# Neighbourhood attention: score products over 128 rows, value products from split operands, summed on the vector engines

## Chip, cores, metric

One core of a Trainium2 chip runs the whole program in one launch. The metric is the device time of one execution, in microseconds (us). Of several runs the median is taken. A profile is one execution recorded by the hardware profiler.

## What is computed

The program computes two layers of a transformer block over 512 image tokens (a grid of 8 rows by 64 columns) and 256 context tokens, with a width of 1024. Each layer has three branches (neighbourhood attention, a pooling mixer, latent attention), a gated merge and a gated feed-forward part. The change touches the neighbourhood branch, which has 8 heads of 64. Every query sees 16 columns of the grid and all 256 context tokens:

```python
s_win = einsum('bjqhd,bkjchd->bhjqkc', q_r, k_nb) * scale
s_win = where(in_win, s_win + bias, -inf)
s_ctx = einsum('bjqhd,bnhd->bhjqn', q_r, k_ctx) * scale
p = softmax(concatenate([s_win, s_ctx], -1))
out = einsum('bhjqkc,bkjchd->bjqhd', p_win, v_nb) + einsum('bhjqn,bnhd->bjqhd', p_ctx, v_ctx)
```

In the first layer the context tokens attend to themselves with the same projections (`dense_attn`). In the second layer their output isn't needed. All arithmetic is float32.

## The kernel before

**Split operands.** Most products run in the type fp32r, in which TensorE reads a float32 operand in reduced form. To keep the accuracy an operand is written as hi + lo: hi is the value rounded to fp32r (a copy on ScalarE, ACT in the profile), lo is the rest (a subtraction on VectorE, DVE, or on GpSimd, POOL). `evac` (line 386) does this for a result in PSUM. A dense product is then three products: hi·lo, hi·hi and lo·hi (`mm3`, line 375).

**The neighbourhood stage** of a layer (lines 936 to 985) works on four pairs of heads p. For each pair, `na_proj` projects queries, values and keys. Each pair has two heads e, on rows 64e to 64e+63 of the 128 partitions. For head e the tile `qz` holds the hi part of the queries on the head's own 64 rows and the lo part on the other 64; `kz` holds the hi part of the keys on both halves; `kl` holds the lo part of the keys of both heads, one head on each half. `na_vt` turns the values (10 blocks of 128 tokens) so that tokens lie on partitions.

**A unit** is one head and one block j of 128 queries (`na_unit`, line 793). Four matmuls make 128 x 512 scores `S`: for each half (window, context) one of `qz` by `kl` over the head's 64 rows alone and one of `qz` by `kz` over 128 rows, which gives hi·hi and lo·hi together. Softmax follows on DVE and ACT, four transposes on TensorE (`tps`), a copy to SBUF on ACT (`PT`), and four plain float32 matmuls of 64 weight columns by 128 moving columns into `ops`. TensorE runs each plain float32 matmul as two recorded passes. All 8 units of a pair write one PSUM tile `ops`, which stays taken until the pair is through; then one `evac` writes `nahi` and `nalo`. There are 32 units in each layer, and 8 units for the context (`na_ctx_unit`, `Sc`, `opc`) in the first.

**Order.** TensorE's order is written when the program is built: `Sched` (line 54) keeps a model of when each operand is ready and interleaves three streams of units (priority 0) with the dense tasks of `dense` (priority 1): the projections of all pairs, the gates and the first compressed projections of latent attention (`cps`). When a unit's next step is not ready by the model, dense matmuls are put in. In the first layer a background stream (`ada_back`, line 430, tile `adacc`) also works on DVE through the whole stage. The orders of the other engines are made by the framework's scheduler. Each engine runs its own order strictly, and waits at an instruction whose operands are missing. PSUM has four one-bank tiles for the units (`p1`) and two double ones for the dense tasks (`mm`). SBUF has `QB` = 12 tiles for queries, keys and values: two pairs of 6.

Of the kernel before, what the change touches and what calls it, by code (L numbers as in the profile page):

```python
# [28 lines left out]
KGAP = 800.0  # L29
QB = 12  # L30
DRATE = 360.0
# [15 lines left out]
class Need:  # L47
    """What a step waits for: tiles that it reads, pools and tags of tiles that it will take."""

# [4 lines left out]
class Sched:  # L54
    """Interleaves generators on the tensor engine by a model of when each step's operands are there."""

# [185 lines left out]
def body(tc, I, out):  # L242
# [247 lines left out]
    def first2(w0, w1, mov, T, dst):  # L490
        """Two weight tiles against the tokens in the order in which these come."""
        ws = (w0.prep(), w1.prep())
        for _ in ws:
            dst.append(pmm.tile([128, 1024], F32, tag="mm", name="f2ps"))
        bounds = [(a, a + 256) for a in range(0, T, 256)]
        n = [0, 0]
        for a, b in bounds:
            tts = range(a // 128, b // 128)
            yield lambda: all(t in tokens for t in tts)
            yield Need(at=max(tokens[t] for t in tts) + sch.HOP)  # L500
            for q in range(2):
# [143 lines left out]
    for l in range(NL):  # L645
# [101 lines left out]
        def na_proj(p, which):  # L747
            def run(w):
# [3 lines left out]
                if which != "v":  # L752
                    z = [na.tile([128, 768], F32R, tag="qkv", bufs=QB, name=which + "z") for _ in range(2)]
                    lo = na.tile([128, 768], F32R, tag="qkv", bufs=QB, name="kl") if which == "k" else None
                    for e in range(2):
                        a, o = slice(64 * e, 64 * e + 64), slice(64 - 64 * e, 128 - 64 * e)
                        for src, place in segs(ps, T):
                            hi = place(z[e])
                            nc.scalar.copy(out=hi[a], in_=src[a])
                            if which == "q":  # L760
                                nc.vector.tensor_sub(out=hi[o], in0=src[a], in1=hi[a].bitcast(F32))
                            else:
                                nc.vector.tensor_sub(out=place(lo)[a], in0=src[a], in1=hi[a].bitcast(F32))
                        if which == "k":
                            nc.scalar.copy(out=z[e][o, :T], in_=z[e][a, :T])
                    qkvt[p, which] = (*z, lo) if lo is not None else tuple(z)
                    return
# [6 lines left out]
        def na_vt(p):  # L774
            def run(_):
                v = qkvt[p, "v"]
                vt = na.tile([128, 10, 128], F32, tag="vt", bufs=2, name="vt")
                srcs = [v[:, 8 * BAND0[j] + 128 * hf:8 * BAND0[j] + 128 * hf + 128] for j in range(4) for hf in range(2)]
                srcs += [v[:, SX + i * 128:SX + (i + 1) * 128] for i in range(2)]
                for i0 in range(0, 10, 4):  # L780
                    tp = ps1.tile([128, 512], F32, tag="p1", name="vtps")
                    n = min(4, 10 - i0)
                    for i in range(n):
                        tr(tp[:, i * 128:(i + 1) * 128], srcs[i0 + i])
                    nc.scalar.copy(out=vt[:, i0:i0 + n, :], in_=tp[:, :n * 128].rearrange("p (k c) -> p k c", k=n))
                qkvt[p, "vt"] = vt
# [4 lines left out]
        biast = {}  # L791

        def na_unit(p, e, j):
            Q, (kk, kl) = qkvt[p, "q"][e], (qkvt[p, "k"][e], qkvt[p, "k"][2])
            vt = qkvt[p, "vt"]
            rows = slice(64 * e, 64 * e + 64)
            if (p, e) not in biast:
                biast[p, e] = na.tile([128, 3, 256], F32, tag="bias", bufs=2, name="bt")
                nc.sync.dma_start(out=biast[p, e], in_=I["rpbg"][l, 2 * p + e])
            if p not in opst:  # L800
                opst[p] = ps1.tile([128, 512], F32, tag="p1", name="ops")
                left[p] = 8
            bt, ops = biast[p, e], opst[p]
            S = ps1.tile([128, 512], F32, tag="p1", name="S")
            for c0 in (0, 256):
                k0 = 8 * BAND0[j] if c0 == 0 else SX
                q = slice(128 * j, 128 * j + 128)
                mm(out=S[:, c0:c0 + 256], lhsT=Q[rows, q], rhs=kl[rows, k0:k0 + 256], start=True, stop=False)
                mm(out=S[:, c0:c0 + 256], lhsT=Q[:, q], rhs=kk[:, k0:k0 + 256], start=False, stop=True)
# [13 lines left out]
            yield Need([P], [P1])  # L823
            tp = transpose_n(P, 4)
            PT = na.tile([128, 512], F32, tag="PT", bufs=3, name="PT")
            nc.scalar.copy(out=PT, in_=tp)
            yield Need([PT])
            for i in range(4):
                iv = 2 * j + i if i < 2 else 6 + i
                mm(out=ops[rows, j * 128:(j + 1) * 128], lhsT=vt[:, iv, rows], rhs=PT[:, i * 128:(i + 1) * 128],  # L830
                   start=i == 0, stop=i == 3)
            left[p] -= 1
            if left[p] == 0:
                evac(ops.rearrange("p (b r c) -> p b r c", b=8, r=8), rowm(nahi[:, p, :SX]), rowm(nalo[:, p, :SX]))
            yield 0

        def na_ctx_unit(p, e):
            Q, (kk, kl) = qkvt[p, "q"][e], (qkvt[p, "k"][e], qkvt[p, "k"][2])
            vt = qkvt[p, "vt"]
            rows = slice(64 * e, 64 * e + 64)  # L840
            S = ps1.tile([128, 512], F32, tag="p1", name="Sc")
            for qt in range(2):
                c, q = slice(qt * 256, (qt + 1) * 256), slice(SX + qt * 128, SX + (qt + 1) * 128)
                mm(out=S[:, c], lhsT=Q[rows, q], rhs=kl[rows, SX:768], start=True, stop=False)
                mm(out=S[:, c], lhsT=Q[:, q], rhs=kk[:, SX:768], start=False, stop=True)
# [11 lines left out]
            yield Need([P], [P1])  # L857
            tp = transpose_n(P, 4)
            PT = na.tile([128, 512], F32, tag="PT", bufs=3, name="PTc")
            nc.scalar.copy(out=PT, in_=tp)  # L860
            yield Need([PT], [P1])
            opc = ps1.tile([128, 512], F32, tag="p1", name="opc")
            for qt in range(2):
                for i in range(2):
                    mm(out=opc[rows, qt * 128:(qt + 1) * 128], lhsT=vt[:, 8 + i, rows],
                       rhs=PT[:, (2 * qt + i) * 128:(2 * qt + i + 1) * 128], start=i == 0, stop=i == 1)
            evac(opc[rows, 0:256], nahi[rows, p, SX:768], nalo[rows, p, SX:768])
            yield 0
# [117 lines left out]

        # latent attention: compressed streams, then the neighbourhood branch joins the sum
        mes = ExitStack()
# [380 lines left out]

        # gated feed-forward  # L1370
        h2 = (mhi, mlo)
# [268 lines left out]
```

## Time and profile before

| | us |
|---|---|
| median of 3 runs (lowest, highest) | 2567.89 (2561.16, 2567.93) |
| span of the profiled execution | 2567.5 |
| TensorE matmuls busy | 2481.2 (97%) |
| DVE busy | 1434.2 (56%) |
| ACT busy | 999.1 (39%) |
| POOL busy | 586.4 (23%) |
| neighbourhood stage, first layer | about 204 to 548 |
| neighbourhood stage, second layer | about 1626 to 1907 |

The busy time of TensorE is the time in which at least one matmul is recorded as running. Matmuls are pipelined, so a single one is listed longer than the step from its start to the start of the next. The cost of a matmul to a busy TensorE is this step, which the timeline shows.

### The profile page before, as it was taken

To read this page: it belongs to the slowest core of one execution; us is meant where nothing else is said; L and a number is where in the kernel's file an instruction comes from. 1 tells how busy PE (TensorE), PEld (TensorE's weight loads), DVE (VectorE), ACT (ScalarE), POOL (GpSimd) and SP (SyncE) were. 2 spreads that over 40 slices of the span, in tenths; PEclk is the share of its full clock that TensorE was granted. 3 is DMA by queue.
4 is the path that set the end of the run, shared out by engine and by line. 5 is a ranking of instruction groups with operands and counts; after the bars stand their busy time and mean duration, and the time that the engine had idled before them with its cause. 6 is when DMAs were issued, how large, how long until landed. Compare 5 with 4: busy or idle time off the path is not lost. (4 is left out here: it accounts for less than half of the span.)

```text
span 2567.5 us, 33598 instructions
## 1 busy us (share of the span) xinstructions
PE 2481.2 (97%) x13060; PEld 2056.5 (80%) x13060; DVE 1434.2 (56%) x2299; ACT 999.1 (39%) x1756; POOL 586.4 (23%) x413
## 2 busy tenths in 40 slices
PE   8899999999999999999999989999999998999998
PEld 6788788788887788888888867877787887888886
DVE  7645544554478668666673475333344785544444
ACT  5213443422467334322222333344423773433332
POOL 4301011142212224222221142101132122222212
PEclk9899999999999999999999999999999999999999
DMA  6343233223333544444431144212124335332322
GB/s 237 103 137 113 77 100 98 97 87 119 110 77 101 193 141 132 134 138 129 135 105 60 51 143 135 98 61 80 62 89 138 100 113 175 125 104 94 99 82 82
DMA packets 98598, 285.91 MB, mean 111 GB/s; under 512 B 12324, under 2 KB 13732, under 8 KB 98440
## 3 DMA queue, kind: packets, MB, share of 16 engines
q1 hardware_dynamic: 98440, 283.78, 34.6%
q8 instruction: 103, 1.69, 0.3%
q14 instruction: 55, 0.45, 0.1%
HBM read 244.34 MB, written 25.23 MB: 105 GB/s over the span
## 5 line engine op out<-in xcount | busy, mean ns | idle before, releaser
L207 ACT CAST whi<-raw 128x1024 fp32r<-128x1024 f32 (+1 forms) x212 | 218.9, 1033 | 501.9 <-PE gps L252 169.5
L207 POOL TENSOR_TENSOR wlo<-raw,whi 128x1024 fp32r<-128x1024 f32 (+2 forms) x81 | 194.6, 2402 | 747.3 <-ACT whi L207 736.7
L207 DVE TENSOR_TENSOR wlo<-raw,whi 128x1024 fp32r<-128x1024 f32 (+1 forms) x131 | 168.8, 1288 | 266.5 <-ACT whi L207 252.3
L252 PE MATMUL ffps<-mhi,whi 128*128 128x512 f32 x1008 | 305.9, 358 | 0.0
L252 PE MATMUL ffps<-mlo,whi 128*128 128x512 f32 x1008 | 305.8, 358 | 0.0
L252 PE MATMUL ffps<-mhi,wlo 128*128 128x512 f32 x1008 | 305.8, 358 | 0.0
L207 DVE SCALAR_TENSOR_TENSOR cv<-ffps,cw,cv 128x511 f32<-128x511 f32 x252 | 161.9, 656 | 133.8 <-ACT cv L207 130.3
L207 DVE SCALAR_TENSOR_TENSOR adacc<-rawa,st,adacc 128x512 f32<-128x512 f32 x224 | 183.9, 847 | 79.4 <-DMA rawa<-in_w_ada 78.0
L252 PEld LDWEIGHTS ffps<-mlo,whi 128*128 128x128 f32 x1008 | 167.6, 189 | 31.8 <-PE ffps L252 0.2
L252 PEld LDWEIGHTS ffps<-mhi,wlo 128*128 128x128 f32 x1008 | 166.6, 189 | 30.3
L252 PEld LDWEIGHTS ffps<-mhi,whi 128*128 128x128 f32 x1008 | 166.6, 189 | 30.2
L252 PE MATMUL dps<-wdl,gh 128*128 128x512 f32 x440 | 174.6, 397 | 2.5 <-DVE y L207 1.4
L252 PE MATMUL dps<-wdh,gl 128*128 128x512 f32 x440 | 175.1, 398 | 0.9 <-POOL gl L207 0.9
L252 PE MATMUL dps<-wdh,gh 128*128 128x512 f32 x440 | 174.1, 396 | 0.0
L207 POOL TENSOR_TENSOR gl<-cv,gh 128x768 fp32r<-128x768 f32 (+1 forms) x44 | 73.1, 1661 | 338.1 <-ACT gh L207 306.4
L207 POOL TENSOR_TENSOR adalo<-adacc,adahi 128x512 fp32r<-128x512 f32 x32 | 45.2, 1411 | 297.8 <-ACT adahi L207 284.3
L207 DVE TENSOR_TENSOR y<-dps,y 128x1024 f32<-128x1024 f32 (+1 forms) x70 | 74.3, 1066 | 59.1 <-PE dps L252 59.1
L256 PE MATMUL tps<-ident,P 128*128 128x128 f32 x672 | 95.9, 274 | 8.9 <-DVE ptl L207 4.4
L252 PEld LDWEIGHTS dps<-wdl,gh 128*128 128x128 f32 x440 | 83.0, 189 | 24.9 <-DVE y L207 1.9
L252 PE MATMUL gps<-hlo,whi 128*128 128x512 f32 (+1 forms) x384 | 100.9, 344 | 0.8 <-DVE craw L207 0.8
L252 PEld LDWEIGHTS dps<-wdh,gl 128*128 128x128 f32 x440 | 82.8, 188 | 20.9 <-POOL gl L207 1.3
L252 PEld LDWEIGHTS dps<-wdh,gh 128*128 128x128 f32 x440 | 82.9, 188 | 20.1
(362 smaller groups left out, 5624.5 us busy)
## 6 DMA issues: line engine op xcount, KB each, us to landing
raw<-in_w_in SPq DMA_DIRECT2D x94, 512.0 KB
raw<-in_w_up SPq DMA_DIRECT2D x88, 512.0 KB
rawa<-in_w_ada SPq DMA_DIRECT2D x80, 512.0 KB
wdr<-in_w_down SPq DMA_DIRECT2D x88, 256.0 KB
raw<-in_w_br SPq DMA_DIRECT2D x24, 512.0 KB
raw<-in_w_ada SPq DMA_DIRECT2D x16, 512.0 KB
wor<-in_w_o SPq DMA_DIRECT2D x32, 256.0 KB
modt<-moda SPq DMA_DIRECT2D x16, 512.0 KB
```

What stands on the lines that cost most here:

```text
L207: r = f(*a, **kw)
L252: nc.tensor.matmul(out=out, lhsT=lhsT, rhs=rhs, start=start, stop=stop)
L256: nc.tensor.transpose(out=out, in_=in_, identity=ident)
```

## The change

- The lo part of the keys gets one tile for each head. DVE writes it on the head's rows, POOL copies it to the other 64. A pair then has 7 tiles, and `QB` becomes 13. Both score matmuls of a half run over 128 rows.
- The turned values and the turned probabilities are kept as hi and lo beside each other: `vt` is 128 weight columns (hi, lo) for each block and head, `PT` 256 moving columns (hi, lo). Four fp32r matmuls give a 128 x 256 result whose four quadrants are the products hi·hi, hi·lo, lo·hi, lo·lo.
- `gather` adds the quadrants for two units at a time: ACT copies the lower 64 rows, DVE adds the upper ones, POOL adds the two column halves, ACT writes `nahi` and DVE `nalo`. The tiles `osum` and `ohead` have one buffer each. `ops` is now held for two units.
- `PT` has 2 buffers, where it had 3. The scratch size for DMAs issued by POOL is set to 1024.

```diff
-QB = 12
+QB = 13
...
-                    lo = na.tile([128, 768], F32R, tag="qkv", bufs=QB, name="kl") if which == "k" else None
+                    lo = [na.tile([128, 768], F32R, tag="qkv", bufs=QB, name="kl") for _ in range(2)] if which == "k" else None
...
-                                nc.vector.tensor_sub(out=place(lo)[a], in0=src[a], in1=hi[a].bitcast(F32))
+                                nc.vector.tensor_sub(out=place(lo[e])[a], in0=src[a], in1=hi[a].bitcast(F32))
                         if which == "k":
                             nc.scalar.copy(out=z[e][o, :T], in_=z[e][a, :T])
+                            nc.gpsimd.tensor_copy(out=lo[e][o, :T], in_=lo[e][a, :T])
...
-                vt = na.tile([128, 10, 128], F32, tag="vt", bufs=2, name="vt")
+                vt = na.tile([128, 10, 2, 2, 64], F32R, tag="vt", bufs=2, name="vt")
...
-                    nc.scalar.copy(out=vt[:, i0:i0 + n, :], in_=tp[:, :n * 128].rearrange("p (k c) -> p k c", k=n))
+                    tv = tp[:, :n * 128].rearrange("p (k e c) -> p k e c", k=n, e=2)
+                    evac(tv, vt[:, i0:i0 + n, :, 0, :], vt[:, i0:i0 + n, :, 1, :])
...
+        def turned(P):
+            tp = transpose_n(P, 4)
+            pt = na.tile([128, 4, 2, 128], F32R, tag="PT", bufs=2, name="PT")
+            evac(tp.rearrange("p (k c) -> p k c", k=4), pt[:, :, 0, :], pt[:, :, 1, :])
+            return pt
+        def weigh(po, vt, e, ivs, pt, i0):
+            for n, iv in enumerate(ivs):
+                mm(out=po, lhsT=vt[:, iv, e].rearrange("p h c -> p (h c)"), rhs=pt[:, i0 + n].rearrange("p h c -> p (h c)"),
+                   start=n == 0, stop=n == len(ivs) - 1)
+        def gather(po, e, hi, lo, shape):
+            t = na.tile([128, 512], F32, tag="osum", bufs=1, name="osum")
+            rows = slice(64 * e, 64 * e + 64)
+            nc.scalar.copy(out=t[0:64], in_=po[64:128])
+            nc.vector.tensor_add(out=t[0:64], in0=po[0:64], in1=t[0:64])
+            v = t[0:64].rearrange("p (u h c) -> p u h c", u=2, h=2)
+            o = na.tile([128, 2, 128], F32, tag="ohead", bufs=1, name="ohead")
+            nc.gpsimd.tensor_add(out=o[rows], in0=v[:, :, 0, :], in1=v[:, :, 1, :])
+            ov = shape(o[rows])
+            nc.scalar.copy(out=hi[rows], in_=ov)
+            nc.vector.tensor_sub(out=lo[rows], in0=ov, in1=hi[rows].bitcast(F32))
...
-                mm(out=S[:, c0:c0 + 256], lhsT=Q[rows, q], rhs=kl[rows, k0:k0 + 256], start=True, stop=False)
+                mm(out=S[:, c0:c0 + 256], lhsT=Q[:, q], rhs=kl[:, k0:k0 + 256], start=True, stop=False)
...
-            PT = na.tile([128, 512], F32, tag="PT", bufs=3, name="PT")
-            nc.scalar.copy(out=PT, in_=tp)
-            yield Need([PT])
-            for i in range(4):
-                iv = 2 * j + i if i < 2 else 6 + i
-                mm(out=ops[rows, j * 128:(j + 1) * 128], lhsT=vt[:, iv, rows], rhs=PT[:, i * 128:(i + 1) * 128],
-                   start=i == 0, stop=i == 3)
+            pt = turned(P)
+            u = (p, e, j // 2)
+            yield Need([pt], [] if u in opst else [P1])
+            if u not in opst:
+                opst[u] = ps1.tile([128, 512], F32, tag="p1", name="ops")
+                left[u] = 2
+            ops = opst[u]
+            weigh(ops[:, (j % 2) * 256:(j % 2 + 1) * 256], vt, e, (2 * j, 2 * j + 1, 8, 9), pt, 0)
+            left[u] -= 1
...
+                gather(ops, e, rowm(nahi[:, p, :SX])[:, c], rowm(nalo[:, p, :SX])[:, c],
+                       lambda x: x.rearrange("p u (b r c) -> p (u b) r c", b=2, r=8))
...
-    nc = bacc.Bacc("TRN2", target_bir_lowering=False, num_devices=1)
+    nc = bacc.Bacc("TRN2", target_bir_lowering=False, num_devices=1, dynamic_dma_scratch_size=1024)
```

`na_ctx_unit` is changed in the same way. Comments and docstrings also went.

On TensorE, a piece of the order in the second pair of the first layer. Before (`ops<-PT,vt` are the value matmuls of one unit, `S<-kl,qz` and `S<-kz,qz` score matmuls of the next, `gps` a dense task; the shapes are those of the results):

```order
L252 MATMUL gps_2653<-hhi_112,wlo_2503 128x512
L252 MATMUL gps_2653<-hhi_112,wlo_2503 128x256
L256 MATMUL tps_2666<-ident_77,P_2594 128x128 x4
L252 MATMUL ops_2541<-PT_2629,vt_2476 64x128 x4
L252 MATMUL S_2677<-kl_2465,qz_2089 128x256
L252 MATMUL S_2677<-kz_2463,qz_2089 128x256
```

Now, at the same place:

```order
L252 MATMUL gps_2795<-hhi_112,wlo_2593 128x512
L252 MATMUL gps_2795<-hhi_112,wlo_2593 128x256
L252 MATMUL ops_2912<-PT_2861,vt_2459 128x256 x4
L252 MATMUL S_2917<-kl_2446,qz_2095 128x256
L252 MATMUL S_2917<-kz_2444,qz_2095 128x256
```

The number of matmul instructions in a unit is the same. The four value matmuls now make 128 x 256 results in place of 64 x 128 ones, and dense work stands between a unit's transposes and its value matmuls as it did before.

On DVE, in the second pair of the first layer, before (`P<-P,rs` is the last step of the softmax, for which the transposes wait; `nalo` the lo part of the stage's result; `sx`, `rs` sums and reciprocals):

```order
L207 TENSOR_REDUCE mx<-S 128x1
L207 TENSOR_TENSOR sx<-sx 128x1
L207 TENSOR_TENSOR nalo<-opc,nahi 64x256
L207 RECIPROCAL rs<-sx 128x1
L207 TENSOR_SCALAR mx<-mx 128x1
L207 TENSOR_SCALAR P<-P,rs 128x512
```

Now, at the like place:

```order
L207 TENSOR_TENSOR PT_2726<-tps_2721,PT_2726 128x4x128
L207 TENSOR_SCALAR mx_2761<-mx_2761 128x1
L207 TENSOR_TENSOR osum_2748<-opc_2743,osum_2748 64x512
L207 ISA P_2782,mx_2783<-S_2777,bt_2615 128x256
L207 ISA mx_2783 128x1
L207 TENSOR_REDUCE mx_2783<-S_2777 128x1
L207 TENSOR_TENSOR sx_2765<-sx_2765 128x1
L207 TENSOR_TENSOR nalo_1739<-ohead_2751,nahi_1738 64x256
L207 RECIPROCAL rs_2769<-sx_2765 128x1
L207 TENSOR_SCALAR mx_2783<-mx_2783 128x1
L207 TENSOR_SCALAR P_2760<-P_2760,rs_2769 128x512
```

The lo part of `PT` and the two DVE steps of `gather` (`osum`, `nalo`) stand among the softmax steps. The row `nalo` waits for `nahi` on ACT, which waits for `ohead` on POOL, which waits for `osum` four rows above; the softmax's last step is behind it.

## Rows read from the trace of the kernel before

**Rows 1.** Page, part 1: engine, busy us (share of the span), instructions.

```profile
PE 2481.2 (97%) x13060; PEld 2056.5 (80%) x13060; DVE 1434.2 (56%) x2299; ACT 999.1 (39%) x1756; POOL 586.4 (23%) x413
```

**Rows 2.** Busy us by stretch: both neighbourhood stages, then pieces of the first.

```profile
core 0: us, PE busy (x) PEld busy (x) DVE busy (x) ACT busy (x) POOL busy (x), PEclk, DMA share, GB/s
204.00:548.00 344.00, 340.55 (x1958) 278.45 (x1957) 176.84 (x432) 139.42 (x321) 51.41 (x32) 1.00 0.30 97
1626.00:1907.00 281.00, 280.14 (x1471) 224.18 (x1472) 94.85 (x276) 116.14 (x258) 37.98 (x20) 0.98 0.24 76
242.00:350.00 108.00, 106.64 (x617) 84.46 (x616) 57.16 (x163) 48.44 (x123) 8.72 (x5) 0.98 0.26 80
350.00:431.00 81.00, 80.92 (x467) 65.91 (x466) 40.91 (x105) 33.84 (x80) 8.80 (x5) 1.00 0.33 103
431.00:504.00 73.00, 70.99 (x415) 57.42 (x414) 38.50 (x100) 32.44 (x77) 11.74 (x6) 1.00 0.27 87
```

**Rows 3.** Timeline of TensorE between two units: start us, us, instructions.

```profile
303.95 1.09 PE L252 MATMUL ops<-PT,vt 128*64 128x128 f32 x8
304.96 0.38 PE L252 MATMUL S<-kl,qz 64*128 64x256 f32 x1
305.27 0.39 PE L252 MATMUL S<-kz,qz 128*128 128x256 f32 x1
...
306.21 1.09 PE L252 MATMUL ops<-PT,vt 128*64 128x128 f32 x8
```

**Rows 4.** Timeline of TensorE in latent attention, value products from split probabilities.

```profile
781.75 0.28 PE L252 MATMUL po<-pth,V 128*128 128x256 f32 x1
781.87 0.28 PE L252 MATMUL po<-ptl,V 128*128 128x256 f32 x1
```

**Rows 5.** Groups by shape, whole span: count, busy us, mean ns, idle before.

```profile
L252 PE MATMUL ops<-PT,vt 128*64 128x128 f32 x512 | 68.8, 279 | 0.0
L252 PE MATMUL S<-kz,qz 128*128 128x256 f32 x128 | 49.7, 388 | 0.0
L252 PE MATMUL S<-kl,qz 64*128 64x256 f32 x128 | 48.9, 382 | 0.0
```

**Rows 6.** The same view, first layer's stage (204 to 548).

```profile
L252 PE MATMUL opc<-PTc,vt 128*64 128x128 f32 x64 | 8.1, 279 | 0.0
```

**Rows 7.** The same view, whole span, of DVE and POOL.

```profile
L207 DVE TENSOR_TENSOR ptl<-tps,pth 128x512 fp32r<-128x512 f32 x104 | 68.4, 681 | 9.6 <-ACT pth L207 9.1
...
L207 POOL TENSOR_TENSOR wlo<-raw,whi 128x1024 fp32r<-128x1024 f32 x76 | 186.5, 2453 | 693.2 <-ACT whi L207 682.6 <-PE S L252 10.0 <-DMA wdr<-in_w_down 0.2
...
L207 POOL TENSOR_TENSOR gl<-cv,gh 128x768 fp32r<-128x768 f32 x22 | 44.2, 2011 | 170.5 <-ACT gh L207 160.4 <-issue 10.0
...
L207 POOL TENSOR_TENSOR rt<-rt 128x256 f32<-128x256 f32 x2 | 1.5, 757 | 4.8 <-DVE rt L207 4.8
```

**Rows 8.** The same view, 242 to 350, of DVE and ACT.

```profile
L207 DVE TENSOR_REDUCE mx<-S 128x1 f32<-128x256 f32 x13 | 5.4, 416 | 0.0
...
L207 DVE TENSOR_TENSOR nalo<-opc,nahi 64x256 fp32r<-64x256 f32 x4 | 1.7, 420 | 0.1
L207 DVE TENSOR_TENSOR nalo<-ops,nahi 128x512 fp32r<-128x512 f32 x2 | 1.4, 691 | 1.9 <-ACT nahi L207 1.9
...
L207 DVE TENSOR_TENSOR qz<-qps,qz 64x512 fp32r<-64x512 f32 x2 | 1.4, 688 | 0.9 <-ACT qz L207 0.9
...
L207 ACT CAST nahi<-opc 64x256 fp32r<-64x256 f32 x4 | 1.5, 367 | 5.0 <-PE opc L252 4.9
```

**Rows 9.** Busy us by stretch, latent attention of both layers (columns as in rows 2).

```profile
690.00:820.00 130.00, 119.13 (x804) 105.03 (x802) 103.83 (x203) 97.97 (x211) 20.09 (x11) 0.99 0.27 66
2000.00:2100.00 100.00, 95.41 (x634) 82.97 (x633) 82.96 (x151) 81.12 (x158) 18.86 (x9) 1.00 0.29 74
```

**Rows 10.** Groups by shape, TensorE, 690 to 820: products over 96 rows and their neighbours.

```profile
L252 PE MATMUL S<-K,Q 128*128 128x256 f32 x72 | 17.3, 285 | 0.0
L252 PE MATMUL S<-K,Q 96*128 96x256 f32 x66 | 15.6, 286 | 0.0
```

More of the change, by code (lines that the diff above doesn't have):

```diff
@@ L762, in run @@
                             else:
-                                nc.vector.tensor_sub(out=place(lo)[a], in0=src[a], in1=hi[a].bitcast(F32))
+                                nc.vector.tensor_sub(out=place(lo[e])[a], in0=src[a], in1=hi[a].bitcast(F32))
                         if which == "k":
                             nc.scalar.copy(out=z[e][o, :T], in_=z[e][a, :T])
-                    qkvt[p, which] = (*z, lo) if lo is not None else tuple(z)
+                            nc.gpsimd.tensor_copy(out=lo[e][o, :T], in_=lo[e][a, :T])
+                    qkvt[p, which] = (*z, *lo) if lo is not None else tuple(z)
                     return
@@ L791, in body @@
         biast = {}
+        def turned(P):
[18 more added lines that the diff above has]
+            nc.vector.tensor_sub(out=lo[rows], in0=ov, in1=hi[rows].bitcast(F32))
         def na_unit(p, e, j):
-            Q, (kk, kl) = qkvt[p, "q"][e], (qkvt[p, "k"][e], qkvt[p, "k"][2])
+            Q, (kk, kl) = qkvt[p, "q"][e], (qkvt[p, "k"][e], qkvt[p, "k"][2 + e])
             vt = qkvt[p, "vt"]
-            rows = slice(64 * e, 64 * e + 64)
             if (p, e) not in biast:
@@ L799, in na_unit @@
                 nc.sync.dma_start(out=biast[p, e], in_=I["rpbg"][l, 2 * p + e])
[L800 to L803, printed above, removed]
+            bt = biast[p, e]
             S = ps1.tile([128, 512], F32, tag="p1", name="S")
@@ L823, in na_unit @@
             yield Need([P], [P1])
-            tp = transpose_n(P, 4)
-            PT = na.tile([128, 512], F32, tag="PT", bufs=3, name="PT")
-            nc.scalar.copy(out=PT, in_=tp)
-            yield Need([PT])
-            for i in range(4):
-                iv = 2 * j + i if i < 2 else 6 + i
-                mm(out=ops[rows, j * 128:(j + 1) * 128], lhsT=vt[:, iv, rows], rhs=PT[:, i * 128:(i + 1) * 128],
-                   start=i == 0, stop=i == 3)
-            left[p] -= 1
-            if left[p] == 0:
-                evac(ops.rearrange("p (b r c) -> p b r c", b=8, r=8), rowm(nahi[:, p, :SX]), rowm(nalo[:, p, :SX]))
+            pt = turned(P)
[7 more added lines that the diff above has]
+            left[u] -= 1
+            if left[u] == 0:
+                c = slice(4 * (j // 2), 4 * (j // 2) + 4)
+                gather(ops, e, rowm(nahi[:, p, :SX])[:, c], rowm(nalo[:, p, :SX])[:, c],
+                       lambda x: x.rearrange("p u (b r c) -> p (u b) r c", b=2, r=8))
             yield 0
         def na_ctx_unit(p, e):
-            Q, (kk, kl) = qkvt[p, "q"][e], (qkvt[p, "k"][e], qkvt[p, "k"][2])
+            Q, (kk, kl) = qkvt[p, "q"][e], (qkvt[p, "k"][e], qkvt[p, "k"][2 + e])
             vt = qkvt[p, "vt"]
-            rows = slice(64 * e, 64 * e + 64)
             S = ps1.tile([128, 512], F32, tag="p1", name="Sc")
@@ L843, in na_ctx_unit @@
                 c, q = slice(qt * 256, (qt + 1) * 256), slice(SX + qt * 128, SX + (qt + 1) * 128)
-                mm(out=S[:, c], lhsT=Q[rows, q], rhs=kl[rows, SX:768], start=True, stop=False)
+                mm(out=S[:, c], lhsT=Q[:, q], rhs=kl[:, SX:768], start=True, stop=False)
                 mm(out=S[:, c], lhsT=Q[:, q], rhs=kk[:, SX:768], start=False, stop=True)
@@ L857, in na_ctx_unit @@
             yield Need([P], [P1])
[L858 to L861, printed above, removed]
+            pt = turned(P)
+            yield Need([pt], [P1])
             opc = ps1.tile([128, 512], F32, tag="p1", name="opc")
             for qt in range(2):
[L864 to L867, printed above, removed]
+                weigh(opc[:, qt * 256:(qt + 1) * 256], vt, e, (8, 9), pt, 2 * qt)
+            gather(opc, e, nahi[:, p, SX:768].rearrange("p (u c) -> p u c", u=2),
+                   nalo[:, p, SX:768].rearrange("p (u c) -> p u c", u=2), lambda x: x)
             yield 0
```

## The prediction

> **What bounds the kernel now.** The page's first part comes first: TensorE has a matmul running for 97% of the span, DVE is busy for 56% [rows 1]. So the order of work on TensorE sets the end, and a change counts by what it does to TensorE's steps and by the waits it puts in between. Next I read the two neighbourhood stages as stretches: in the first layer 340.55 of 344 us, in the second 280.14 of 281 us have a matmul running [rows 2]. TensorE waits for 3.5 and 0.9 us there, so chains of softmax work are hidden behind dense matmuls. DVE has 51% and 34% of these stretches [rows 2]. "Busy" doesn't say that TensorE is quick, so the third view is the timeline of one unit [rows 3]. The reader is to see two things in it. The four score matmuls start 0.31 us apart, from 304.96 to 306.21, which is 1.25 us for the four. The eight passes of the four value matmuls take from 303.95 to 304.96, 1.01 us. For comparison, latent attention has matmuls of the same 256 moving columns with other weights each time, all over 128 rows: they start 0.12 us apart [rows 4].
>
> **TensorE's part of the change.** Units: 512 passes of `ops` are 64 units of 8, 64 passes of `opc` are 8 more [rows 5, 6], 72 in all, 40 in the first layer and 32 in the second. The score matmuls stay 4 in a unit (128 and 128 in the 64 grid units [rows 5]).
>
> - Scores: what is different between the two rows is that `S<-kl,qz` uses 64 rows and `S<-kz,qz` 128, in turn. With 128 rows throughout, I take the step of rows 4: 4 x 0.12 = 0.48 us in place of 1.25, a gain of 0.77 us in a unit, 72 x 0.77 = 55.4 us. Bounds: nothing (0.31 stays) to these 55.4.
> - Values: four matmuls of 256 moving columns in fp32r with 128 weight columns are the very form of rows 4: 0.48 us in place of 1.01, 72 x 0.53 = 38.2 us. The row is that of the same operation, so this term is firm.
>
> Sum on TensorE: -93.6 us, which is 1.30 us in each unit.
>
> [...]
>
> **What it adds elsewhere.** DVE, by rows of the same kind:
>
> - The lo part of the turned probabilities: 72 x 0.681 (`ptl`, the same operation [rows 7]) = 49.0 us.
> - The lo part of `vt`, 8 pairs x (2 x 0.681 + 0.42) = 14.3 us.
> - 40 gathers (32 of the grid, 8 of the context), each an addition of 64 x 512 from PSUM, as 64 x 512 of `qz` at 0.688, and a subtraction of 64 x 256 at 0.420 [rows 8]: 44.3 us.
> - Gone: 8 x 0.691 and 8 x 0.420 of `nalo` [rows 8], 8.9 us.
>
> Together +98.7 us, 54.8 of them in the first layer (40 units, 4 pairs, 24 gathers) and 43.9 in the second. ACT gains a copy of 64 x 512 and one of 64 x 256 in a gather; with 0.367 us for the smaller [rows 8] and under twice that for the larger this is under 44 us, on an engine that has 139 and 116 us in the stages [rows 2]. It costs nothing in itself. POOL gains 40 additions of 64 x 256, by a row of 128 x 256 at 0.757 us 30 us, and 16 copies of 64 x 768 for `kl`. A copy is not in the trace; it lies between 0.76 (the row of 128 x 256) and 2.01 us (128 x 768 from two operands [rows 7]), and I take 2.0 by the equal number of columns. That is 62 us on an engine that has 51 and 38 us in the stages. The copies make the keys of a pair ready 2 to 4 us later (up to 6.5 with one weight split of 2.45 us ahead of them on POOL [rows 7]); the next pair's projections or gates are in TensorE's order there, so this is hidden in every pair but perhaps the first. No more wait is priced for the 13 tiles: the seventh tile of the next pair takes the place of `qz` of head 0, whose last scores stand ahead of the end of that projection in the order. The smaller DMA scratch is free here: SP issues every DMA that the page lists.
>
> **What of it comes onto the path.** Before, dense matmuls covered the softmax. After, a unit takes TensorE 1.30 us less, and DVE 1.2 to 1.4 us more. I set the two against each other by stretch in the first layer, where the background stream also uses DVE.
>
> - 242 to 350: 20 units end in it (2 pairs and their context units, by `nalo` x2 and x4 [rows 8]). DVE: 57.2 + 20 x 0.681 + 1.8 + 12 x 1.108 - 3.1 = 82.8 us. TensorE: 108 - 20 x 1.30 = 82.0 us. DVE is late here.
> - 350 to 431: 10 units. DVE 40.9 + 13.7 = 54.6 us, TensorE 81 - 13 = 68 us.
> - 431 to 504: 10 units. DVE 38.5 + 13.7 = 52.2 us, TensorE 73 - 13 = 60 us.
>
> [...] The highest share of DVE over a like stretch in this trace is in latent attention: 83% in the second layer, 80% in the first, where TensorE goes without work for 4.6 of 100 and 10.9 of 130 us [rows 9]. If DVE gets no further than 83%, the three stretches need 99.8, 65.8 and 62.9 us, so TensorE waits 17.8, 0 and 2.9 us more. In the second layer DVE comes to 94.9 + 43.9 = 138.8 us in 281 - 32 x 1.30 = 239 us, 58%; at 51% the first layer had 3.5 us of waits before, so I put 3 there. New waits: 24 us. Bounds: 0 (all of it hidden) and 45 us (latent attention's 8.4% over both stages, 531 us).
>
> [...]
>
> **Sum.** 2567.5 - 93.6 + 24 = 2497.9 us. The span of the profiled execution is 0.4 us under the median of the runs (2567.9), so the forecast is 2498 us, a gain of 2.7%.
>
> **Rivals.**
>
> - *All of it is gained.* TensorE's order keeps other units' and dense matmuls between the steps of a unit, as before, and waits stay near their 4 us: 2567.5 - 93.6 + 0 to 10 = 2474 to 2484 us. For it: the waits before are small. Against it: 82.8 us of DVE in 82.
> - *DVE takes the lead for good.* The upper bound of waits, and on top some of the gathers' stalls (next rival, at a third of its price): 2567.5 - 93.6 + 45 + 0 to 35 = 2519 to 2554 us. For it: in the order DVE's `nalo` waits for ACT, ACT for POOL, and the softmax's last step stands behind it, on which the transposes wait. Against it: the second layer has room.
> - *Rows don't matter.* The 0.31 us have another cause (the turn between hi and lo keys, or the weights not loaded ahead), and only the values gain: 2567.5 - 38.2 + 5 to 10, about 2537 us. Against it: latent attention's scores alternate between 128 and 96 rows, and a 256-column one is listed at 285 and 286 ns, where those of this stage are listed at 388 and 382 [rows 5, 10]. A turn of weights or of row counts alone isn't dear.
> - *Slower: the gather stalls DVE.* `osum` and `ohead` have one buffer, and POOL may be in a weight split. Then `nalo` comes after 2.45 + 0.76 + 0.37 = 3.58 us [rows 7, 8], and the score steps that stand between cover about two of 0.42 us, so DVE stops for 2.7 us, and a softmax behind it. Were that so at each of 40 gathers and all on TensorE's path, 108 us: 2497.9 + 108 = 2606 us. It decides from (93.6 - 24) / 40 = 1.7 us at each gather. Against it: POOL has about 86 (51.4 + 24 x 0.76 + 8 x 2.0) of 290 us of work in the first layer's stage, so some three in ten gathers meet a busy POOL, 0.8 us on average, and part of these fall where dense work covers.
>
> **How the numbers follow.** Chances: the forecast with waits of 10 to 45 us, 2484 to 2519: 0.55. All gained, 0.17. DVE in the lead, 0.20. Rows don't matter, 0.04. Gather stalls to slower, 0.03; 0.01 for what isn't seen here. A measurement of this kernel tells a change from none at about 0.3%, 8 us. Faster by more than that: all but the gather case and the rest, 0.95; within 0.3%: 0.02; slower: 0.03. The range takes in the forecast, most of the first rival and the larger part of the second: 2476 to 2533 us.
>
> **What would show it.** The timeline should have four `S` steps of 0.12 us and four `ops` steps of 0.12 us; if `S` stays at 0.31, the third rival holds. The first layer's stage should shrink from 344 to about 314 us and the second's from 281 to about 243. DVE should be above 75% busy between the first pair's keys and the last pair's units, and TensorE's new idle time there should end by DVE (`P<-P,rs` ahead of `tps`, `PT` ahead of `ops`). If those waits lie behind `nalo` and POOL's `ohead`, the gather is the reason. The forecast is wrong if waits come to under 10 or over 45 us, or if stages that aren't touched move by more than a few us.

## The result and the profile after

The changed kernel takes 2495.0 us (median of 4 runs, 2489.3 to 2502.2), beside 2564.5 us of the kernel before on the same chip. The ratio is 0.9729, with a 95% interval of 0.9706 to 0.9753. The forecast was 2498 us, the range 2476 to 2533.

Page, part 1, of the changed kernel (as rows 1):

```profile
PE 2389.7 (96%) x12772; PEld 2012.9 (81%) x12772; DVE 1539.8 (62%) x2456; ACT 1030.8 (41%) x1820; POOL 639.8 (26%) x472
```

Its span is 2495.7 us, 71.8 less than before. The two neighbourhood stages, taken from the first query projection to the end of `krps` behind them, are 203.9 to 557.1 and 1626.6 to 1907.3 us before, 205.9 to 529.3 and 1594.9 to 1835.6 now: 29.8 and 40.0 us shorter. The rest of the span is 2.0 us shorter. The stages of the kernel before, by the same ends (columns as in rows 2):

```profile
203.90:557.10 353.20, 349.75 (x2011) 286.52 (x2010) 181.54 (x438) 141.64 (x324) 53.32 (x33) 1.00 0.30 97
1626.60:1907.30 280.70, 280.44 (x1473) 224.43 (x1474) 94.30 (x275) 115.76 (x259) 37.98 (x20) 0.98 0.24 76
```

The stretches of the changed kernel, its two stages and then three pieces of the first, cut so that 20, 10 and 10 units end in them as in the three pieces of the prediction:

```profile
205.90:529.30 323.40, 302.76 (x1847) 266.23 (x1846) 228.84 (x510) 159.83 (x359) 88.75 (x67) 0.98 0.31 103
1594.90:1835.60 240.70, 234.93 (x1345) 201.78 (x1346) 140.66 (x347) 128.90 (x287) 55.52 (x44) 1.00 0.27 88
...
242.00:348.00 106.00, 94.96 (x590) 83.60 (x589) 86.99 (x214) 63.62 (x155) 21.62 (x18) 0.97 0.27 86
348.00:419.00 71.00, 66.63 (x418) 58.63 (x416) 53.76 (x124) 38.02 (x90) 19.72 (x15) 1.00 0.31 103
419.00:495.00 76.00, 70.76 (x430) 61.96 (x429) 57.88 (x127) 38.12 (x86) 24.28 (x16) 0.98 0.29 94
```

The reader is to subtract the second number from the first: TensorE without a matmul for 20.6 and 5.8 us, where it was 3.5 and 0.3 in the same two stages before. The busy time fell by 47 and 46 us. The granted clock went from 1.00 to 0.98 in the first stage and from 0.98 to 1.00 in the second. What a lower clock costs shows at 255.4 to 257.4 us of the changed kernel: at a granted 0.50 the pairs of dense matmuls of 512 and 256 columns start 0.64 us apart, at 259.2 to 260.6, at 1.00, 0.35. By estimate that is about 6 us more in the first stage (0.02 of 303) and 6 us less in the second (0.02 of 280), so the clock's part nearly cancels.

The timeline of TensorE in the changed kernel, at the end of one unit and the scores of the next (as rows 3):

```profile
288.34 0.64 PE L252 MATMUL ops<-PT,vt 128*128 128x256 f32 x4
288.81 0.28 PE L252 MATMUL S<-kl,qz 128*128 128x256 f32 x1
288.93 0.29 PE L252 MATMUL S<-kz,qz 128*128 128x256 f32 x1
289.06 0.28 PE L252 MATMUL S<-kl,qz 128*128 128x256 f32 x1
289.17 0.28 PE L252 MATMUL S<-kz,qz 128*128 128x256 f32 x1
289.33 0.74 PE L252 MATMUL opc<-PT,vt 128*128 128x256 f32 x4
```

Four value matmuls take 0.47 us (1.01 before), four score matmuls from 288.81 to 289.33, 0.52 us (1.25 before). The waits of TensorE in the first stage, by what ended them (us in total, times, longest):

```profile
PE S L252 <- DVE mx L207: 5.0, 4, 2.0
PE tps L256 <- ACT P L207: 4.2, 3, 2.4
PE ops L252 <- DVE PT L207: 3.4, 4, 1.9
PE opc L252 <- DVE PT L207: 3.0, 2, 2.8
```

`mx`, which the first row names, is a small row in SBUF. At three of its four waits (4.4 of the 5.0 us) the row right ahead of it on DVE is the lo copy `PT<-tps`, which reads the PSUM tile of the transposes. That `S` waits for this tile to come free is likely, and not shown by a run.

The rows of the added work, whole span (count, busy us, mean ns, idle before and its end):

```profile
L207 DVE TENSOR_TENSOR PT<-tps,PT 128x512 fp32r<-128x512 f32 x72 | 48.3, 684 | 13.5 <-ACT PT L207 13.1
...
L207 DVE TENSOR_TENSOR nalo<-ohead,nahi 64x256 fp32r<-64x256 f32 x40 | 18.5, 463 | 19.9 <-ACT nahi L207 19.5
...
L207 POOL TENSOR_TENSOR ohead<-osum 64x256 f32<-64x256 f32 x40 | 34.0, 849 | 206.4 <-DVE osum L207 164.6 <-DVE rs L207 18.5 <-DVE sx L207 13.8
L207 POOL CAST kl<-kl 64x768 fp32r<-64x768 f32 x16 | 13.2, 822 | 24.0 <-DVE kl L207 23.6
```

### The profile page after: what moved, and what is told of

The parts are those of the page before. It is cut to its first block, busy times and chain, and to the rows that moved or that the text cites. A ratio compares the mean times of both kernels' runs of the same rounds, so it can differ in the third digit from the quotient of the medians.

```text
span 2495.7 us, 33312 instructions
## 1 busy us (share of the span) xinstructions
PE 2389.7 (96%) x12772; PEld 2012.9 (81%) x12772; DVE 1539.8 (62%) x2456; ACT 1030.8 (41%) x1820; POOL 639.8 (26%) x472
## 5 line engine op out<-in xcount | busy, mean ns | idle before, releaser
L207 POOL TENSOR_TENSOR wlo<-raw,whi 128x1024 fp32r<-128x1024 f32 (+2 forms) x84 | 203.4, 2421 | 526.7 <-ACT whi L207 495.6
L207 DVE SCALAR_TENSOR_TENSOR adacc<-rawa,st,adacc 128x512 f32<-128x512 f32 x224 | 190.9, 880 | 63.4 <-DMA rawa<-in_w_ada 61.6
L207 DVE TENSOR_TENSOR y<-dps,y 128x1024 f32<-128x1024 f32 (+1 forms) x70 | 74.3, 1066 | 59.1 <-PE dps L252 58.9
L252 PE MATMUL gps<-hhi,whi 128*128 128x512 f32 (+1 forms) x384 | 99.5, 341 | 0.0
L252 PE MATMUL gps<-hhi,wlo 128*128 128x512 f32 (+1 forms) x384 | 99.1, 339 | 0.0
```

Of the source, the lines that this page charges most:

```text
L207: r = f(*a, **kw)
L252: nc.tensor.matmul(out=out, lhsT=lhsT, rhs=rhs, start=start, stop=stop)
```

## Experiments

Two questions were open. Is it the turn between 64 and 128 rows that made the scores slow? And why does TensorE wait 23 us more: because DVE has too much to do (*load*), or because of what stands ahead of a unit's own steps on DVE and in its chain (*order and chain*)? Whenever the program is built, the orders of all engines are made anew, so most experiments change more than the lines shown; where TensorE's order stayed the same, the text says so. Times are medians with the ratio to the kernel before on the same chip; the changed kernel is at 0.9729.

**e1, scores alone.** The kernel before with the key and score parts of the change (the three edits on `lo`, `QB`, and both score matmuls over 128 rows).

```diff
-lhsT=Q[rows, q], rhs=kl[rows, k0:k0 + 256]
+lhsT=Q[:, q], rhs=kl[:, k0:k0 + 256]
```

> Kernel before with the score products alone changed (two tiles of low key parts, POOL copies, 13 tiles, all score matmuls over 128 rows); the value products stay plain float32. Theory (the 0.31 us step comes from 64-row products standing among 128-row ones): S steps fall to 0.12 us, TensorE's steps lose 55 us, DVE's load does not grow (57% busy in the stage), so hardly a wait comes back: about 53 us below before, 2510 to 2516. Rival (rows do not matter, the gain of the whole change came from the values): within 5 us of before. Second rival (the late key copies on POOL cost waits): 2518 to 2530.

Measured: 2514.6 us, 0.9787 [0.9765, 0.9809], 52 us gained by the medians. The stages of e1:

```profile
204.30:532.90 328.60, 323.81 (x2011) 277.88 (x2010) 183.54 (x439) 140.46 (x324) 56.43 (x40) 1.00 0.30 104
1599.10:1854.40 255.30, 254.31 (x1473) 214.30 (x1474) 101.98 (x282) 115.61 (x259) 27.66 (x21) 1.00 0.24 83
```

A unit of e1 on the timeline of TensorE:

```profile
297.77 1.09 PE L252 MATMUL ops<-PT,vt 128*64 128x128 f32 x8
298.79 0.39 PE L252 MATMUL S<-kl,qz 128*128 128x256 f32 x1
299.01 0.28 PE L252 MATMUL S<-kz,qz 128*128 128x256 f32 x1
299.13 0.28 PE L252 MATMUL S<-kl,qz 128*128 128x256 f32 x1
299.24 0.28 PE L252 MATMUL S<-kz,qz 128*128 128x256 f32 x1
299.45 0.76 PE L252 MATMUL ops<-PT,vt 128*64 128x128 f32 x5
```

The steps between scores are 0.12 us; the first and the last, beside the 64-column `ops`, are 0.22 and 0.21. TensorE waits 4.8 and 1.0 us, 2 us more than before. The scores are the larger part of the gain, and hardly anything of it comes back.

**e2, values alone.** The changed kernel with the 64-row scores put back (and with them one `kl` tile for a pair and 12 tiles).

```diff
-lhsT=Q[:, q], rhs=kl[:, k0:k0 + 256]
+lhsT=Q[rows, q], rhs=kl[rows, k0:k0 + 256]
```

> The changed kernel with the score products put back (one tile of low key parts, 12 tiles, 64-row products among 128-row ones); the value products split as in the change. Theory (waits come from DVE having less of TensorE's time to hide behind): TensorE's steps lose 38 us and DVE gains its 99 us, but each unit keeps 0.77 us more of TensorE, so that waits are about 8 us in place of the 23 that came with both: 2530 to 2536. Rival (the waits come from the longer chain of each unit alone, whatever TensorE has to do): all 23 us stay, 2547 to 2552.

Measured: 2543.9 us, 0.9893 [0.9864, 0.9921], 23 us gained by the medians. The stages of e2:

```profile
204.00:550.50 346.50, 335.53 (x1849) 278.49 (x1848) 232.95 (x514) 160.81 (x360) 75.94 (x57) 0.97 0.28 96
1621.20:1886.00 264.80, 260.71 (x1345) 211.31 (x1346) 139.27 (x348) 129.97 (x287) 46.13 (x35) 0.99 0.24 80
```

Waits of 11.0 and 4.1 us, 11 more than before in place of the expected 8 and not 23. The time lies between both expectations; the granted clock of 0.97 in the first stage has a part in it, by estimate up to 10 us (0.03 of 335.5). Alone, the scores bring 2 us of waits (e1) and the values 11; together they bring 23. So the two parts together make waits that neither makes alone, with another TensorE order in each of these kernels.

**e3, fewer turns.** The kernel before, with the two score products of the first half in the other order, so that two 64-row products are neighbours.

```diff
+two = [(Q[:, q], kk[:, k0:k0 + 256]), (Q[rows, q], kl[rows, k0:k0 + 256])]
+for n, (a, b) in enumerate(two if c0 == 0 else two[::-1]):
+    mm(out=S[:, c0:c0 + 256], lhsT=a, rhs=b, start=n == 0, stop=n == 1)
```

> Kernel before with the order of each unit's four score products changed from low, high, low, high to high, low, low, high, so that two 64-row products stand next to each other: two turns between 64 and 128 rows in a unit in place of four. Theory (the turn costs about 0.19 us, not the row count): two steps of each unit fall from 0.31 to 0.12 us, 72 x 0.38 = 27 us less, 2535 to 2540. Rival (a 64-row product is slow by itself, or the weights of the other tile are): all steps stay at 0.31, no change.

Measured: 2541.3 us, 0.989 [0.9872, 0.9908], 26 us gained by the medians (27 expected) with the same products over the same rows, and with DVE's and ACT's order in both stages as before. A unit of e3 on the timeline of TensorE:

```profile
302.27 0.38 PE L252 MATMUL S<-kz,qz 128*128 128x256 f32 x1
302.59 0.50 PE L252 MATMUL S<-kl,qz 64*128 64x256 f32 x2
303.02 0.38 PE L252 MATMUL S<-kz,qz 128*128 128x256 f32 x1
303.24 0.40 PE L252 MATMUL gps<-hlo,whi 128*128 128x512 f32 x1
```

The two 64-row products together take 0.43 us (302.59 to 303.02), where two took 0.62 before. Each has a turn on one side now and takes about 0.21. A 128-row product with a turn on one side (303.02 to 303.24) takes 0.22 as well, and the first one, which stands between the 64-column `ops` and a 64-row product, 0.32. So a step is 0.12 us without a turn (128-row products), and for either kind about 0.21 with a turn on one side and 0.31 with one on both: a turn costs 0.19 us and shows half on either side. The rival, that 64 rows are slow in themselves, falls. How the time of a turn is spent no run shows.

**e4, background without loads to wait for.** The changed kernel; the background's multiply-adds read a resident tile.

```diff
-w = raw[:, (k % 2) * 512:(k % 2 + 1) * 512]
+w = rope_c[:, 0:512]
```

> The changed kernel, in which the background stream's multiply-adds on DVE read a tile that is in SBUF since the start in place of the loaded weights (the loads are still issued); the modulation of the norms is then not computed from its weights. DVE's load is the same, but it never waits at one of these rows for a load to land (24 us of idle time in the first layer's stage of the changed kernel). Theory load (waits in the first stage come from DVE's busy share): TensorE's waits there stay at 15 to 22 us, time within 5 us of the changed kernel. Rival head (they come from DVE standing at a background row while a unit's row is behind it): waits fall to 5 to 12 us and the time by 8 to 14 us, to about 2483.

Measured: 2500.1 us, 0.9734 [0.9715, 0.9752]. First stage of e4:

```profile
199.70:528.10 328.40, 302.54 (x1847) 266.33 (x1846) 225.83 (x506) 159.97 (x359) 91.50 (x67) 0.98 0.30 102
```

TensorE waits 25.9 us, more than either theory expected, though its order in this stage is that of the changed kernel, matmul by matmul, and DVE's waits for these loads (24.0 us in the changed kernel) are gone. So DVE standing at a load isn't what makes up the waits. What e4 can't say is that it costs nothing, since DVE's order moved too: 14 of the multiply-adds now stand in one run from 203.0 to 215.7, and 3.8 us of the waits are new ones, at `kps` behind `qz`.

**e5, no background.** The changed kernel with 2 of the 16 rows of a chunk on DVE (its first product for each of two sequences), read from a resident tile.

```diff
-for k in (2 * q, 2 * q + 1):
-    w = raw[:, (k % 2) * 512:(k % 2 + 1) * 512]
+for k in ((0,) if q == 0 else ()):
+    w = rope_c[:, 0:512]
```

> The changed kernel, in which the first layer's background stream loads its weights but leaves out all but one of the 16 multiply-adds of each chunk (the modulation of the norms is then not computed). DVE loses about 35 us of work in the first layer's neighbourhood stage, 194 in place of 229. Theory load (waits there come from DVE having about as much to do as TensorE): TensorE's waits in that stage fall from about 21 to 6 to 12 us and the time by 10 to 15 us from the changed kernel, to about 2483. Rival (each unit's longer chain, not the sum of DVE's work): waits stay at 18 or more, time within 5 us of 2495.

**e6, no gather.** The changed kernel without the sums.

```diff
-nc.scalar.copy(out=t[0:64], in_=po[64:128])
-nc.vector.tensor_add(out=t[0:64], in0=po[0:64], in1=t[0:64])
...
-nc.gpsimd.tensor_add(out=o[rows], in0=v[:, :, 0, :], in1=v[:, :, 1, :])
-ov = shape(o[rows])
+ov = shape(po[rows, 0:256].rearrange("p (u c) -> p u c", u=2))
```

> The changed kernel without the sums of the gather: ACT and DVE write hi and lo straight from one part of the PSUM result (the other quadrants are left out of the result). No osum, no ohead, nothing on POOL, no row on DVE that waits for ACT behind POOL; DVE loses 40 x 0.69 = 27 us, 17 of them in the first layer. Theory load: 17 us less of DVE's work brings the first stage's waits from 21 to about 12 us, time about 2486. Rival gather (waits come mostly from the serial gather holding DVE and the PSUM tile): both stages' waits fall to what they were before, 4 us and less, time about 2475.

**e7, no lo part of the probabilities.** The changed kernel with two fixed tiles and zeros in the lo half.

```diff
-evac(tp.rearrange("p (k c) -> p k c", k=4), pt[:, :, 0, :], pt[:, :, 1, :])
...
+pt = pts[(len(turns) - 1) % 2]
+nc.scalar.copy(out=pt[:, :, 0, :], in_=tp.rearrange("p (k c) -> p k c", k=4))
```

> The changed kernel without the lo part of the turned probabilities: two fixed tiles whose lo half is zero, ACT writes the hi half (the product with the lo part is left out). DVE loses 72 x 0.68 = 49 us, 27 in the first layer, and a unit's chain loses a step on DVE, so that the PSUM tile of the transposes comes free 0.7 us earlier. Theory load: waits of the first stage fall from 21 to 6 to 10 us, and the second stage's hardly move (5.8 to 3 to 5). Rival chain (the step on DVE between transposes and value products is the reason wherever it is): both fall to nothing, time about 2472.

Measured: e5 2478.3 us, 0.9658 [0.9641, 0.9674]; e6 2495.3 us, 0.9724 [0.9707, 0.9741]; e7 2483.8 us, 0.9677 [0.9661, 0.9693]. The first stage of e5:

```profile
196.40:509.30 312.90, 299.60 (x1847) 265.41 (x1846) 181.26 (x440) 158.94 (x358) 82.14 (x66) 0.99 0.31 107
```

Both stages of e6:

```profile
206.60:527.60 321.00, 302.10 (x1851) 267.06 (x1850) 206.10 (x489) 144.45 (x336) 67.87 (x44) 0.98 0.30 103
1592.90:1834.30 241.40, 234.42 (x1345) 201.80 (x1346) 125.74 (x331) 118.47 (x270) 44.55 (x28) 1.00 0.26 88
```

Both stages of e7:

```profile
201.00:516.20 315.20, 301.55 (x1851) 266.46 (x1850) 207.59 (x476) 158.03 (x360) 87.05 (x67) 0.98 0.31 105
1580.90:1819.00 238.10, 234.42 (x1345) 202.10 (x1346) 120.71 (x319) 128.11 (x286) 51.60 (x42) 1.00 0.26 89
```

All three miss what either theory expected of the first stage's waits. e6 and e7 take about the same off DVE (23 and 21 us less in the first stage, 15 and 20 in the second). e6 leaves the waits at 18.9 and 7.0 us and gains no time; e7 brings them to 13.7 and 3.7 and gains 11 us. e5 brings DVE to the 181 us that it had before the change, and TensorE still waits 13.3 us, beside 3.5 before. So the sum of DVE's work alone doesn't set the waits, and about 13 us remain without the background as well as without the lo part.

What the 7 us are that e5 and e7 each take off is less clear. In e5 TensorE's order is nearly that of the changed kernel (one group of `vps` and two of `cps` moved), but the run doesn't tell the background's work from its place. In e6 and e7 TensorE's order is another one, and in e7 ACT's waits at `PT` for the value matmuls (below) are gone too. That the lo part costs by its place, between the transposes and the value matmuls, is argued and not shown. Of the gather e6 shows no part, in time (the ratio of the changed kernel) or in waits, though under another TensorE order.

One of these waits, on DVE of the changed kernel (timeline: start us, us):

```profile
365.79 2.73 DVE L207 SCALAR_TENSOR_TENSOR adacc<-rawa,st,adacc 128x512 f32<-128x512 f32 x3
368.55 0.42 DVE L207 CUSTOM_DVE_ANT_0 P<-S,bt 128x256 f32<-128x256 f32 x1
...
371.43 0.49 DVE L207 TENSOR_SCALAR P<-P,rs 128x512 f32<-128x512 f32 x1
```

and the transposes that wait for it, on TensorE:

```profile
369.13 0.51 PE L252 MATMUL gps<-hhi,wlo 128*128 128x512 f32 x2
372.06 0.63 PE L256 MATMUL tps<-ident,P 128*128 128x128 f32 x4 [2.42 <-ACT P L207]
```

Three background rows keep DVE from 365.79 to 368.52, and only then come the steps of three units' softmax. TensorE has put its dense matmuls behind it by 369.6 and stands for 2.42 us.

**A rival that no run tested: two buffers for `PT`.** The change also took `PT` from 3 buffers to 2. ACT's waits at `PT` in the first stage, before and then in the changed kernel:

```profile
ACT PT L207 <- PE tps L256: 24.2, 15, 4.9
...
ACT PT L207 <- PE ops L252: 20.8, 8, 3.7
ACT PT L207 <- PE tps L256: 6.0, 7, 2.4
```

Before, the copy to `PT` never waited for value matmuls (`ops`) to release a buffer. In the changed kernel it does so eight times, and still does in e5 (18.9 us) and e9 (20.4 us). Only one of the eight, at 460.25, is also what DVE's lo copy then waits for, with 0.47 us on TensorE behind it; at the others DVE is at other rows up to the lo copy. But the orders were made for two buffers, and no run has three, so how much of the waits is due to this stays open.

**e9, priority.** The changed kernel with the copies of the turned probabilities at the softmax's priority.

```diff
-evac(tp.rearrange("p (k c) -> p k c", k=4), pt[:, :, 0, :], pt[:, :, 1, :])
+with tc.high_priority(HP):
+    evac(tp.rearrange("p (k c) -> p k c", k=4), pt[:, :, 0, :], pt[:, :, 1, :])
```

> The changed kernel with the two copies of the turned probabilities (hi on ACT, lo on DVE) put at the same high priority as the softmax, so that they stand ahead of weight splits, background and gather rows in the orders. Same work. Theory load: DVE's sum is the same in the stretches where it is short, so waits fall by at most a third, time 2488 to 2496. Rival (order on DVE, not its sum): waits of the first stage fall from 21 to 10 or less, time below 2485.

Measured: 2491.2 us, 0.9708 [0.9693, 0.9723]. The first stage of e9:

```profile
201.40:520.10 318.70, 302.54 (x1847) 266.55 (x1846) 226.44 (x509) 158.75 (x359) 86.99 (x67) 0.98 0.30 104
```

The stage's waits fall to 16.2 us with about the same work on DVE. That is less than the theory of order expected, and within what the theory of load allowed. But TensorE's order is that of the changed kernel, matmul by matmul, so these 4.5 us do come from the order on DVE and ACT. In the time alone e9 isn't told from the changed kernel, since the intervals overlap.

**e11, e12 and e13, the background's order.** e11: the changed kernel with the multiply-adds one at a time; e12: that and e9; e13: that, and the background's pace set by stage.

```diff
-                yield pace
+                        yield (pace[0] if isinstance(pace, list) else pace) / (2 * ns)
...
+    pace0 = [5000.0]
...
+        pace0[0] = 24000.0
...
+        pace0[0] = 8000.0
```

The second value holds in the first stage, the third behind it.

> The changed kernel with the background stream's multiply-adds put into the order one at a time in place of four together, the same work at the same pace. After the runs before: leaving the gather's sums out took 23 us of DVE's work from the first stage and 2 us of its waits, leaving the lo part of the probabilities out took 21 us and 7 us, leaving the background out took 47 us and 7 us. So DVE's sum is not what counts. Theory order (rows that stand ahead of a unit's step on DVE, background rows in blocks of 3 us, and the lo part in the unit's chain): waits of the first stage fall from 21 to 14 to 17 us, time 2488 to 2492. Rival load: no change of waits, 2495.

> Both: turned probabilities at high priority (which alone took the first stage's waits from 21 to 16 us), background multiply-adds one at a time. Theory order: waits of the first stage 10 to 14 us, time 2484 to 2490. Rival load: as with the priority alone, 2491.

> As the one before, and the background stream runs at a pace of 5 us a quarter ahead of the first neighbourhood stage, 24 us in it and 8 us behind it (12 throughout before): the same work, most of it moved out of the stage, where leaving it out took 7 us of waits and 4 to 6 us of the pooling stage ahead. Theory order: first stage's waits 8 to 12 us; ahead of the stage its loads compete with the weights, so that up to 5 us can be lost there: 2478 to 2488, the fastest version that leaves nothing out. Rival (the loads and multiply-adds are dearer where they go to): over 2492.

Measured: e11 2507.5 us, 0.9765 [0.9737, 0.9793]; e12 2495.8 us, 0.9723 [0.9697, 0.975]; e13 2497.6 us, 0.9731 [0.9709, 0.9753]. All three miss the times expected. The first stages of e11 and e12:

```profile
197.20:522.10 324.90, 302.58 (x1847) 267.58 (x1846) 219.94 (x501) 160.44 (x359) 85.17 (x67) 0.98 0.29 97
197.80:517.20 319.40, 302.58 (x1847) 266.67 (x1846) 218.12 (x501) 158.84 (x359) 85.53 (x67) 0.98 0.29 99
```

e11 waits 22.3 us, but it doesn't test what it was made for: on DVE seven runs of four background rows are left in the stage, where the changed kernel has eight, because DVE's order is made by the framework's scheduler. Whether blocks of rows count stays open. e12 waits 16.8 us, where 10 to 14 were expected. It has e11's TensorE order in the stage and its work on DVE to 2 us, so the priority takes off 5.5 us here, as it took off 4.5 in e9. These few us aren't scatter between executions: in the second stage, where the changed kernel, e5 and e11 have the same order on TensorE and on DVE, their waits are 5.8, 5.7 and 5.7 us. The part between the stages, which has a background of its own in the feed-forward part, became longer (1079 us in e11, 1084 in e13, 1066 in the changed kernel, from the stages' ends). The pace of e13 did what was expected of it in the stage, where 11.8 us of waits are left:

```profile
201.00:510.60 309.60, 297.82 (x1840) 263.47 (x1840) 208.35 (x479) 155.91 (x355) 75.27 (x61) 0.99 0.27 91
```

**e14, priority and pace, blocks of four.** e9 with the pace by stage.

```diff
-                yield pace
+                yield pace[0] if isinstance(pace, list) else pace
...
+    pace0 = [6000.0]
...
+        pace0[0] = 24000.0
...
+        pace0[0] = 12000.0
```

> The changed kernel with the turned probabilities at high priority and the first background stream at a pace of 6 us a quarter ahead of the first neighbourhood stage, 24 us in it, 12 us behind it; its multiply-adds in blocks of four, since putting them one at a time cost 12 to 14 us in the feed-forward part. Theory order: first stage as in the run before with this pace (waits 10 to 14 us, 310 to 314 us long), the part between the stages back at 1065 to 1071 us: 2476 to 2485, faster than the changed kernel. Rival (what the background gains in the stage it loses ahead of it, where 4 us more of waits were seen): over 2489.

Measured: 2475.5 us, 0.9649 [0.9636, 0.9662], faster than the changed kernel by 20 us and clear of its interval. It leaves nothing out. The waits of its first stage, 12.3 us, are as expected, the time a little below the 2476 to 2485 us. Its stages:

```profile
197.20:504.80 307.60, 295.28 (x1843) 262.13 (x1842) 201.18 (x477) 156.99 (x356) 81.49 (x63) 1.00 0.26 91
1574.00:1814.10 240.10, 235.24 (x1345) 201.83 (x1346) 138.65 (x347) 127.85 (x286) 55.42 (x44) 1.00 0.26 88
```

The first stage is 15.8 us shorter than in the changed kernel: 8.3 us fewer waits, and 7.5 us less busy time, part of it, by estimate about 6 us (0.02 of 302.8), by a clock of 1.00 in place of 0.98. The part ahead of the stage is 8.7 us shorter, but the first stage begins at 196 to 207 us across these runs, and at 201.4 in e9, whose edit touches nothing ahead of it, where the changed kernel has 205.9. How much of these 8.7 us is the pace stays open. The part between the stages is 3.6 us longer.

## Why the prediction was right, and where not

- **The score step** was right. Both numbers hold: 0.31 us before and 0.12 after, by the turns (e3). The two terms of the sum aren't independent, though: `ops` over 64 columns is a turn as well (score steps of 0.22 and 0.21 us beside it in e1), and a turn's price lies half on either side, so that e1 and e2 don't split the gain just as the terms did. Their sum was right: -92.5 us of busy time in the two stages, predicted -93.6. A 64-row and a 128-row product take nearly the same step where both have a turn on one side (0.21 and 0.22 us in e3); what is above 0.12 us there is the turn's half on that side. One reading behind the step was wrong: latent attention's scores over 96 and over 128 rows don't alternate, they stand in runs of one kind. At the four places between 690 and 820 us where the two meet without a wait, the step across is 0.12 us all the same, so the argument against the third rival stands.
- **DVE's added work** was 105.6 us over the span, predicted 98.7. The copies of `kl` on POOL were mis-sized: 0.82 us, where I took 2.0. The addition on POOL took 0.85, where I took 0.76.
- **The waits** had the right size: 22.7 us more in the two stages, predicted 24. But the step that gave it failed: "If DVE gets no further than 83%" put 17.8, 0 and 2.9 us into three stretches of the first stage. With as many units ending in them (and more dense work in the first) these show 11.0, 4.4 and 5.2 us without a matmul, with DVE at 82, 76 and 76%. DVE's 83% isn't what sets the waits: they come at 76% too (4.4 us where the step gave none), e5 keeps 13 us of them at DVE's old load, and e9 and e12 take off 4.5 and 5.5 us with the same matmul order and nearly the same work on DVE. The size came out by luck. A part of what makes it is the order on DVE and ACT; that the unit's longer chain is the rest is argued. The third `PT` buffer was given up in the change, and the prediction didn't price it.
- **The sign for the waits** held in part. They end by DVE or by the softmax, and not behind `nalo`, but the largest single group is of `S` (5.0 us), which the prediction hadn't named.
- **Gather as a danger** fell. DVE does wait for ACT at `nalo` (19.5 us in all), but leaving the sums out (with another TensorE order) moved neither the median nor a stage's waits by more than 2 us.
- **The second layer** was right: 46.4 us of new work on DVE (43.9 predicted), 5.5 us of new waits (3 predicted).

What stays open is the 12 to 14 us of waits that remain in the first stage in e5, e7 and e14, each time with other rows at their end. Four PSUM banks serve scores, transposes and sums of three streams, and some waits of `S` end just behind a DVE row that reads such a bank (three in the changed kernel's first stage, 4.4 us). No run changed the number of banks or of `PT` buffers.

## What to carry to other kernels

Look at the steps between the starts of neighbouring matmuls, not at their listed durations or at a busy share: TensorE was busy for over 98% of both stages before, and yet the score rows alone gave 52 us (e1), because products over 64 and over 128 rows stood in turn. Filling unused rows with data that does no harm (e1), or putting products over equally many rows side by side (e3, 26 us), took away turns here at no cost on TensorE that either run shows. When work then goes to other engines, look beyond their sum: the same work in another order on DVE and ACT waited 4.5 to 5.5 us less (e9, e12). And when an experiment's orders are made anew with it, compare the orders themselves before naming a cause.

## What was not expected of the hardware

The price of a turn lies on both neighbours. A 128-row product beside a 64-row one takes 0.21 to 0.22 us in e3 in place of 0.12, so the kind of a slow matmul doesn't tell what slows it. And the values' plain float32 matmuls over 64 columns had turns of their own: from their last pass to the next score is 0.20 us in e1, where a pass within takes 0.11. Whether the 64 columns or the type makes this turn no run tells apart.
